# Two chained matmuls with a GELU: the first slices of b loaded by another queue, and the order of the first loads

## The chip, the cores and the metric

The kernel runs on one core of a Trainium2 chip. The metric is the device time of one execution in microseconds. Three runs of the kernel before gave 117.23, 117.33 and 117.46 us, so the median is 117.33.

Five engines work side by side, each through its own list of instructions: TensorE (PE, with its weight loads shown apart as PEld), VectorE (DVE), ScalarE (ACT), GpSimd (POOL) and SyncE (SP). Transfers from the chip's memory (DRAM) are issued by SP and POOL here, and moved by 16 DMA engines.

## The reference

```python
m, k, n, p = 1024, 1024, 2048, 1024
h = np.matmul(a, b)            # a: 1024 x 1024, b: 1024 x 2048, float32
h = 0.5 * h * (1 + np.tanh(np.sqrt(2 / np.pi) * (h + 0.044715 * h ** 3)))
return np.matmul(h, c).astype(np.float32)      # c: 2048 x 1024
```

## The kernel before

Everything is computed in bf16 or in a rounded fp32 form (FP32R) with fp32 sums in PSUM. The order of the work on each engine is written out by hand.

**Stages.** The first 512 columns of b are multiplied with a in the plain way: this is the loading stage, in which the data arrive (L114). The next 512 columns of b (`zero`), the last 1024 (`one`) and the whole second product with c (`two`) are each computed by a scheme with seven block products in place of eight (`Seven`, L212), whose sums and differences DVE forms (L170). GELU is applied by ACT as it takes the sums out of PSUM (L118).

**The loading stage.** a is needed transposed, with the contraction index on the partitions. It comes in pieces `a_part(h, q)`: h is the half of the rows, q one of four groups of 256 columns, 512 KB each in fp32. Of b's first 512 columns there are eight slices k, 256 KB each; `b_part(q)` is slices 2q and 2q + 1.

- `cast_a` (L128) casts a piece to bf16 with the engines it is given, each one share of the columns. `turn` (L138) transposes a piece, eight times 128 x 128 on PE by means of the matrix `ident` (L145), into PSUM, and DVE copies each of the two results into `aT` (L146). It is a generator: `next(tn)` does one half. `cast_b` (L149) casts a slice of b into `b1`, `block` (L156) issues the matmuls of L114, and `stir` (L122) issues matmuls on zeros, which nobody reads.
- SP issues, in this order: a(0,0) into `sta` (L75), b's slices 0 and 1 into `stb` (L76), a(1,0) (L77), a(0,1) (L78), b's slice 2 (L79). These arrive as fp32 and are cast by DVE and ACT.
- POOL first builds `ident` (L51), then copies one element of a(0,0) into `gate` (L81), which holds it until that piece has landed. Then it issues all other loads, which cast from fp32 to bf16 on the way: a(1,1) (L91), b's slice 3 (L92), a(0,2), b's slices 4 and 5, a(1,2), a(0,3), b's slices 6 and 7, a(1,3) (L86 and L89), then the rest of b (L98, L101) and c (L104). From the ninth on, each waits until the load eight places earlier has landed.
- ACT runs one GELU on a constant into the tile `g` (L82), so that its table is loaded early.

**The first work on PE** (L229 to L242): five stirs; the first half of a(0,0)'s transposes, a stir, the second half, a stir; then the matmuls of b's slice 0 with four column tiles and of slice 1 with two; then a(1,0)'s transposes, and so on. Between those, slices 0 and 1 of b are cast (L233, L236): slice 0 by DVE, DVE and ACT, slice 1 by ACT.

**The end.** The second product's results go out by `store` (L428), called in `done2` (L431); one tile of them goes out in two halves (L436).

Of the kernel before, what the change touches and what calls it, by code (L numbers as in the profile page):

```python
# [9 lines left out]
F32 = mybir.dt.float32  # L10
F32R = mybir.dt.float32r
BF16 = mybir.dt.bfloat16
AF = mybir.ActivationFunctionType
# [6 lines left out]
def kernel(ctx, tc, a, b, c, out):  # L20
    nc = tc.nc
    M, K = a.shape
    _, N = b.shape
    _, P = c.shape
    H = 512
# [8 lines left out]
    consts = ctx.enter_context(tc.tile_pool(name="consts", bufs=1))  # L34
# [5 lines left out]
    def slot(tag, shape, dt, name):  # L40
        return big.tile(shape, dt, name=name, tag=tag)

    def bank(i, shape=(128, H), dt=F32, name="ps"):
        return pp.tile(list(shape), dt, name=name, tag=f"bank{i}", padded_shape=None)

    def pieces(tag, bufs, shape, dt, name):
        return small.tile(shape, dt, name=name, tag=tag, bufs=bufs)

    warm = nc.const_aps.tensor(0.0, [128, 256], F32)
    ident = consts.tile([128, 128], BF16, name="ident")  # L50
    make_identity(nc, ident)  # L51
    gate = consts.tile([128, 1], F32, name="gate")
    g = consts.tile([128, 1], F32, name="g")

    consts.tile([128, 16], F32, name="room")

    c_sb = keep.tile([128, NT, P], BF16, name="c_sb")
    hT = [keep.tile([128, NT, H], BF16, name=f"hT{h}") for h in range(2)]
# [1 line left out]
    b1 = slot("b1", [128, KT, 1024], BF16, "b1")  # L60
# [4 lines left out]
    stb = slot("x0", [128, KT, H], F32, "stb")  # L65
    sta = slot("x1", [128, 2, 2, 4, 256], F32, "sta")
    abq = slot("x3", [128, 4, 2, 4, 256], BF16, "abq")

    def a_part(h, q):
        return av[:, 4 * h:4 * h + 4, ds(q * 256, 256)]  # L70

    def b_part(q):
        return bv[:, 2 * q:2 * q + 2, 0:H]

    nc.sync.dma_start(out=sta[:, 0, 0], in_=a_part(0, 0))  # L75
    nc.sync.dma_start(out=stb[:, 0:2], in_=b_part(0))  # L76
    nc.sync.dma_start(out=sta[:, 1, 0], in_=a_part(1, 0))  # L77
    nc.sync.dma_start(out=sta[:, 0, 1], in_=a_part(0, 1))  # L78
    nc.sync.dma_start(out=stb[:, 2], in_=bv[:, 2, 0:H])  # L79

    nc.gpsimd.tensor_copy(gate, sta[:, 0, 0, 3, 0:1])  # L81
    nc.scalar.activation(g, warm[:, 0:1], AF.Gelu_apprx_tanh)  # L82


    def cast_load_a(h, q):
# [13 lines left out]
    for n in range(2):  # L99
        for k in range(0, KT, 4):  # L100
            nc.gpsimd.dma_start(out=b2[:, k:k + 4, ts(n, H)],  # L101
                                in_=bv[:, k:k + 4, ds(1024 + n * H, H)])
# [3 lines left out]
    def copy(eng, dst, src):  # L106
        if eng is nc.scalar:
            nc.scalar.activation(dst, src, AF.Copy)
        else:
            nc.vector.tensor_copy(dst, src)  # L110
# [11 lines left out]
    def stir(*widths):  # L122

        for w in widths:
            nc.tensor.matmul(ps[0, 3][:, 0:w], warm[:, 0:128], warm[:, 0:w],
                             start=True, stop=True, skip_group_check=True)

    def cast_a(h, q, *engs):  # L128

        ab = pieces("ab", 2, [128, 4, 256], BF16, "ab")  # L130
        for i, eng in enumerate(engs):
            w = 256 // len(engs)
            for j, e in enumerate(eng if isinstance(eng, tuple) else (eng,)):
                m = slice(2 * j, 2 * j + 2) if isinstance(eng, tuple) else slice(0, 4)
                copy(e, ab[:, m, ts(i, w)], sta[:, h, q][:, m, ts(i, w)])
        return ab

    def turn(h, q, i, ab):  # L138

        banks = i if isinstance(i, tuple) else (i,)  # L140
        pts = [bank(x, (128, 2, H), BF16, "pt") for x in banks]
        for n in range(2):
            pt = pts[n % len(pts)]
            for m in range(4):
                nc.tensor.transpose(pt[:, n, ts(m, 128)], ab[:, m, ts(n, 128)], ident)  # L145
            nc.vector.tensor_copy(aT[:, h, 2 * q + n], pt[:, n])  # L146
            yield

    def cast_b(k, *engs):  # L149
        c0 = 0  # L150
        for i, eng in enumerate(engs):
            w = (H - c0) if i == len(engs) - 1 else H // len(engs) // 128 * 128
            copy(eng, b1[:, k, ds(c0, w)], stb[:, k, ds(c0, w)])
            c0 += w
# [72 lines left out]
    one = Seven(4, quarters(b2, 0, H), BB, [None] * 4, zero.t)  # L227

    stir(256, 256, 256, 256, 256)  # L229
    tn = turn(0, 0, 4, cast_a(0, 0, nc.vector))  # L230
    next(tn)
    stir(128)
    cast_b(0, nc.vector, nc.vector, nc.scalar)  # L233
    next(tn)
    stir(64)
    cast_b(1, nc.scalar)  # L236
    ab = cast_a(1, 0, nc.vector, nc.scalar)
    block(0, range(4), (0,))
    block(0, range(2), (1,))
# [9 lines left out]
    tn = turn(0, 1, 7, ab)  # L249
# [4 lines left out]
    for q in range(1, 3):  # L254
        k = 2 * q
        block(0, range(4), (k,))
        tn = turn(1, q, 7, abq[:, q, 1])
# [5 lines left out]
        tn = turn(0, q + 1, 7, abq[:, q + 1, 0])  # L263
# [10 lines left out]
    tn = turn(1, 3, 0, abq[:, 3, 1])  # L274
# [153 lines left out]
    def store(mt, q0, w, ot, eng=None):  # L428
        (eng or nc.sync).dma_start(out=out[ts(mt, 128), ds(q0, w)], in_=ot)

    def done2(i, l, j, p):  # L431
        if (i, l) == (1, 0):
            ot = pieces("o", 4, [128, H], F32, "ot")
            nc.vector.tensor_copy(ot, p)
            p = ot
        n = 2 if (i, l, j) == (0, 0, 1) else 1  # L436
        for q in range(n):
            r = ds(q * (H // n), H // n)
            store(4 * i + j, l * H + q * (H // n), H // n, p[:, r])

    def between2(n):
# [12 lines left out]
        elif n == "P73":  # L454
            two.t4(two.t[1], 4)

    seven(two, done2, between2)


# [28 lines left out]
```

## Time and profile before

| | |
|---|---|
| median of three runs | 117.33 us |
| the profiled execution | 117.6 us |
| its span, first to last instruction | 115.8 us |
| PE busy | 110.7 us, 96% of the span |
| DVE busy | 90.1 us, 78% |
| ACT busy | 51.4 us, 44% |
| POOL busy | 17.3 us, 15% |
| granted clock of TensorE | 1.00 throughout |
| read from DRAM, written to it | 20.97 MB, 4.19 MB |
| loads by SP and POOL, us from issue to landing | a(0,0), a(1,0) and a(0,1): 6.2 (median of the three); b's slices 0 and 1: 5.4; the five casting loads of a: 8.0 (median) |

Times in the profile are in microseconds from the start of the span. A busy PE says little, since matmuls are pipelined and their ends are modelled. What matters is where PE stands still, what released it, and when the loads that released it were issued and landed. The rate of the transfers in the profile counts bytes written: a load that casts from fp32 to bf16 reads twice what it writes. Queue q1 holds SP's transfers, q0 those of POOL, q8 fetches of instructions.

### The profile page before, as it was taken

To read this page: it belongs to the slowest core of one execution; us is meant where nothing else is said; L and a number is where in the kernel's file an instruction comes from. 1 tells how busy PE (TensorE), PEld (TensorE's weight loads), DVE (VectorE), ACT (ScalarE), POOL (GpSimd) and SP (SyncE) were. 2 spreads that over 40 slices of the span, in tenths; PEclk is the share of its full clock that TensorE was granted. 3 is DMA by queue.
4 is the path that set the end of the run, shared out by engine and by line. 5 is a ranking of instruction groups with operands and counts; after the bars stand their busy time and mean duration, and the time that the engine had idled before them with its cause. 6 is when DMAs were issued, how large, how long until landed. Compare 5 with 4: busy or idle time off the path is not lost.

```text
span 115.8 us, 1473 instructions
## 1 busy us (share of the span) xinstructions
PE 110.7 (96%) x544; PEld 77.1 (67%) x550; DVE 90.1 (78%) x108; ACT 51.4 (44%) x86; POOL 17.3 (15%) x29
## 2 busy tenths in 40 slices
PE   7889999999999999999999999999999999999990
PEld 6545555445777447888886444588888888888870
DVE  0247747689999998944789999999999986964581
ACT  5053000799268998066699339700043992000000
POOL 2497754222332000000000000000000000000000
PEclk9999999999999999999999999999999999999999
DMA  3999999999999999998000000070000002004994
GB/s 74 296 381 221 200 199 204 204 207 207 205 210 210 211 212 212 212 210 163 9 0 0 6 0 0 0 272 0 0 0 0 0 0 94 2 27 173 364 358 166
DMA packets 13414, 15.94 MB, mean 138 GB/s; under 512 B 736, under 2 KB 9184, under 8 KB 13408
## 3 DMA queue, kind: packets, MB, share of 16 engines
q0 software_dynamic: 8672, 9.31, 47.6%
q1 hardware_dynamic: 4592, 6.42, 15.7%
q10 hardware_dynamic: 144, 0.13, 0.3%
q8 instruction: 4, 0.07, 0.2%
q14 instruction: 2, 0.02, 0.0%
HBM read 20.97 MB, written 4.19 MB: 217 GB/s over the span
## 4 chain that ended last, share of the span: by engine, by line
PE 79%; DMA 13%; POOL 5%; issue 0%; DVE 0%
PE ps L212 76%; DMA abq<-in_a_dram 10%; DMA sta<-in_a_dram 3%; POOL abq L86 3%; PE ps L114 2%; POOL b L89 1%; POOL gate L81 1%; PE pt L145 1%; POOL b L92 0%; DVE ot L375 0%
## 5 line engine op out<-in xcount | busy, mean ns | idle before, releaser
L212 PE MATMUL ps<-x,s 128*128 128x512 f32 x128 | 29.6, 391 | 0.0
L212 PEld LDWEIGHTS ps<-x,s 128*128 128x128 f32 x128 | 24.0, 188 | 5.1
L212 PE MATMUL ps<-x,x 128*128 128x512 f32 x96 | 22.9, 394 | 0.0
L212 PEld LDWEIGHTS ps<-x,x 128*128 128x128 f32 x96 | 18.0, 188 | 3.9
L114 PE MATMUL ps<-aT,b 128*128 128x512 bf16 x62 | 15.7, 379 | 0.3 <-DVE b L110 0.2
L298 ACT ACTIVATE v<-ps 128x512 f32<-128x512 f32 x10 | 6.0, 598 | 19.1 <-PE ps L212 19.1
L212 PE MATMUL ps<-c_sb,hT 128*128 128x512 bf16 (+2 forms) x78 | 14.1, 336 | 0.1
L212 PE MATMUL ps<-x 128*128 128x512 f32 x56 | 13.2, 393 | 0.0
L212 PEld LDWEIGHTS ps<-x 128*128 128x128 f32 x56 | 10.2, 188 | 2.7 <-ACT u L298 0.4
L212 PEld LDWEIGHTS <-hT 128*128 128x128 bf16 x80 | 7.1, 98 | 7.0 <-issue 0.5
L118 ACT ACTIVATE hT<-ps 128x512 bf16<-128x512 f32 x14 | 7.3, 596 | 9.6 <-PE ps L114 9.6
L118 ACT ACTIVATE hT<-ot 128x512 bf16<-128x512 f32 x18 | 10.4, 623 | 2.1 <-DVE ot L303 2.0
L146 DVE COPY aT<-pt 128x512 bf16<-128x512 bf16 x16 | 6.7, 422 | 5.5 <-PE pt L145 5.4
L212 PE MATMUL ps<-aT,b 128*128 128x512 bf16 x46 | 10.6, 379 | 0.1
L303 DVE TENSOR_TENSOR ot<-ps,u 128x512 f32<-128x512 f32 x10 | 6.7, 688 | 5.2 <-ACT u L298 5.2
L303 DVE TENSOR_TENSOR ot<-ps,v 128x512 f32<-128x512 f32 x10 | 6.7, 688 | 4.9 <-DMA out_dram<-ot 3.9
L170 DVE TENSOR_TENSOR x<-c_sb 128x1024 fp32r<-128x1024 bf16 x8 | 9.2, 1216 | 0.0
L114 PEld LDWEIGHTS <-b 128*128 128x128 bf16 x64 | 5.7, 97 | 4.5 <-DVE b L110 0.3
L212 PEld LDWEIGHTS <-b 128*128 128x128 bf16 x48 | 4.6, 97 | 5.7 <-issue 0.3
L104 POOL DMA_DIRECT2D c_sb<-in_c_dram x8 | 5.6, 703 | 13.4 <-DMA b<-in_b_dram 11.1
L170 DVE TENSOR_TENSOR x<-b 128x1024 fp32r<-128x1024 bf16 (+1 forms) x4 | 7.0, 1751 | 0.6 <-issue 0.6
L298 ACT ACTIVATE u<-ps 128x512 f32<-128x512 f32 x10 | 5.9, 597 | 3.4 <-PE ps L212 3.2
(44 smaller groups left out, 110.7 us busy)
## 6 DMA issues: line engine op xcount, KB each, us to landing
c_sb<-in_c_dram POOLq DMA_DIRECT2D x8, 512.0 KB, 19.7
out_dram<-ot SPq DMA_DIRECT2D x14, 256.0 KB, 2.1
b<-in_b_dram POOLq DMA_DIRECT2D x6, 512.0 KB, 15.6
sta<-in_a_dram SPq DMA_DIRECT2D x3, 512.0 KB, 6.2
abq<-in_a_dram POOLq DMA_DIRECT2D x5, 256.0 KB, 8.0
stb<-in_b_dram SPq DMA_DIRECT2D x1, 512.0 KB, 5.4
b<-in_b_dram POOLq DMA_DIRECT2D x2, 256.0 KB, 8.3
stb<-in_b_dram SPq DMA_DIRECT2D x1, 256.0 KB, 7.2
```

The lines of the kernel that those rows point to most:

```text
L81: nc.gpsimd.tensor_copy(gate, sta[:, 0, 0, 3, 0:1])
L86: nc.gpsimd.dma_start(out=abq[:, q, h], in_=a_part(h, q))
L89: nc.gpsimd.dma_start(out=b1[:, 2 * q:2 * q + 2, 0:H], in_=b_part(q))
L104: nc.gpsimd.dma_start(out=c_sb[:, t:t + 2], in_=cv[:, t:t + 2])
L114: nc.tensor.matmul(p, b1[:, k, ts(t, 128)], aT[:, h, k], start=(k == 0), stop=(k == KT - 1))
L118: nc.scalar.activation(hT[h][:, t], p, AF.Gelu_apprx_tanh)
L145: nc.tensor.transpose(pt[:, n, ts(m, 128)], ab[:, m, ts(n, 128)], ident)
L146: nc.vector.tensor_copy(aT[:, h, 2 * q + n], pt[:, n])
L170: nc.vector.tensor_tensor(out=dst[:, r], in0=x[:, r], in1=y[:, r], op=op)
L212: nc.tensor.matmul(p[:, ds(c0, w)], l[:, k, ts(j, 128)], r[:, k, ds(c0, w)], start=(start and k == 0), stop=(k == self.kt - 1), skip_group ...
L298: nc.scalar.activation(st, p, AF.Copy)
L303: nc.vector.tensor_tensor(out=ot, in0=p, in1=st, op=ADD)
```

## The change

Slices 0 and 1 of b are no longer loaded by SP as fp32 and cast by DVE and ACT: POOL issues their load, with the cast, as its first instruction, ahead of `ident`. SP's second load is then a(1,0). ACT's early GELU writes its one element into the place that a(1,0) will fill, so that SP issues that load only when ACT is done; the tile `g` is gone, and `room` is one element larger. a(0,0) is cast half by DVE and half by ACT, its eight transposes follow each other into two banks of PSUM, and the two small stirs come behind them. Two of the tiles of the second product go out in halves instead of one.

```diff
-    make_identity(nc, ident)
     gate = consts.tile([128, 1], F32, name="gate")
-    g = consts.tile([128, 1], F32, name="g")
-
-    consts.tile([128, 16], F32, name="room")
+
+    consts.tile([128, 17], F32, name="room")
...
+    nc.gpsimd.dma_start(out=b1[:, 0:2, 0:H], in_=b_part(0))
+    make_identity(nc, ident)
     nc.sync.dma_start(out=sta[:, 0, 0], in_=a_part(0, 0))
-    nc.sync.dma_start(out=stb[:, 0:2], in_=b_part(0))
+    nc.scalar.activation(sta[:, 1, 0, 0, 0:1], warm[:, 0:1], AF.Gelu_apprx_tanh)
     nc.sync.dma_start(out=sta[:, 1, 0], in_=a_part(1, 0))
     nc.sync.dma_start(out=sta[:, 0, 1], in_=a_part(0, 1))
     nc.sync.dma_start(out=stb[:, 2], in_=bv[:, 2, 0:H])
 
     nc.gpsimd.tensor_copy(gate, sta[:, 0, 0, 3, 0:1])
-    nc.scalar.activation(g, warm[:, 0:1], AF.Gelu_apprx_tanh)
...
     stir(256, 256, 256, 256, 256)
-    tn = turn(0, 0, 4, cast_a(0, 0, nc.vector))
-    next(tn)
-    stir(128)
-    cast_b(0, nc.vector, nc.vector, nc.scalar)
-    next(tn)
-    stir(64)
-    cast_b(1, nc.scalar)
+    for _ in turn(0, 0, (4, 5), cast_a(0, 0, nc.vector, nc.scalar)):
+        pass
+    stir(128, 64)
     ab = cast_a(1, 0, nc.vector, nc.scalar)
...
-        n = 2 if (i, l, j) == (0, 0, 1) else 1
+        n = 2 if (i, l) == (0, 0) and j else 1
```

## The prediction

> **What bounds the kernel now.** I read the chain of waits first. It says that PE ends the span, and which transfer PE last waited for.
>
> ```profile
> 10.15 11.43 DMA abq<-in_a_dram
> 21.58 0.05 issue
> 21.63 0.40 PE pt L145 x4
> ...
> 73.79 39.11 PE ps L212 x188
> ```
>
> Columns: start, duration, what. Nothing but PE stands on the chain from 21.63 us on, with "issue" gaps of 0.05 us. The change moves nothing behind that point except one split store, so it must be read from when PE can start the transposes of a's last piece, abq(1,3), at 21.63.
>
> Next the timeline of the loading stage: start, duration, engine, line, and in brackets the idle time before and its releaser.
>
> ```profile
> 0.74 0.42 SPq L75 DMA_DIRECT2D sta<-in_a_dram  x1
> 1.77 0.46 SPq L77 DMA_DIRECT2D sta<-in_a_dram  x1
> 2.04 0.20 ACT L82 ACTIVATE g<-const-float32-0.0 128x1 f32<-128x1 f32 x1
> 4.46 0.69 DVE L110 CAST ab<-sta 128x1024 bf16<-128x1024 f32 x1 [4.46 <-DMA sta<-in_a_dram]
> 5.14 0.88 POOL L86 DMA_DIRECT2D abq<-in_a_dram  x1
> 6.62 0.94 ACT L108 ACTIVATE b<-stb 128x256 bf16<-128x256 f32 x2 [4.38 <-DMA stb<-in_b_dram]
> 6.90 1.47 PE L114 MATMUL ps<-aT,b 128*128 128x512 bf16 x6 [0.17 <-DVE b L110]
> 7.99 0.43 DVE L110 CAST ab<-sta 128x512 bf16<-128x512 f32 x1 [0.68 <-DMA sta<-in_a_dram]
> 7.99 0.63 ACT L108 ACTIVATE ab<-sta 128x512 bf16<-128x512 f32 x1 [0.44 <-DMA sta<-in_a_dram]
> 8.47 0.62 PE L145 MATMUL pt<-ident,ab 128*128 128x128 bf16 x8
> 15.99 0.24 PEld L145 LDWEIGHTS <-abq 128*128 128x128 bf16 x4 [0.30 <-DMA abq<-in_a_dram]
> 21.62 0.23 PEld L145 LDWEIGHTS <-abq 128*128 128x128 bf16 x4 [0.64 <-DMA abq<-in_a_dram]
> ```
>
> PE's first real matmul is at 6.90. Two later places show PE waiting for data that this change does not reorder: abq(1,2) at 15.99 (PE had just become free, no loss) and abq(1,3) at 21.62. Single starts put PE's last matmul before the second at 21.10; at the pace of 0.217 us between them PE was free at 21.32, so this wait costs 0.31 us.
>
> So **an earlier start of PE alone is worth nothing**: PE would arrive earlier at 15.99 and 21.62 and wait for the same landings. Only a load stream that ends earlier moves the end. Third, then, the stretches: length, five engines busy (count), PE's clock, DMA share, GB/s written.
>
> ```profile
> 2.50:4.25 1.75, 1.75 (x6) 1.37 (x6) 0.00 (x0) 0.00 (x0) 0.00 (x0) 1.00 1.09 347
> 4.25:5.50 1.25, 0.82 (x8) 0.42 (x6) 0.69 (x1) 0.00 (x0) 1.01 (x2) 1.00 0.87 238
> 6.00:8.50 2.50, 2.10 (x13) 1.07 (x13) 1.19 (x5) 1.45 (x3) 2.50 (x5) 1.00 1.08 384
> 10.00:19.00 9.00, 8.90 (x68) 5.06 (x70) 5.89 (x13) 0.72 (x2) 5.51 (x9) 1.00 1.38 199
> ```
>
> From 10 us on POOL's queue casts fp32 to bf16, so 199 written is 398 read. The stream runs at 384 to 398 read from about 2.5 to the end, except for a **dip** to 238 between 4.25 and 5.50: it loses 1.25 x (384 - 238)/384 = 0.48 us. The packets of the dip are those of b's first two slices (2 KB each, SP's queue).
>
> **The change part by part.**
>
> *b's first slices through POOL's queue.* Removed: SP's issue (L76, 0.50 us) and the four casts of L110 and L108 (DVE 0.36, ACT 0.94). Added: one POOL issue ahead of ident; L89 has the same shape and takes 0.73. POOL goes through it from 0.74 to 1.47, and ident's two instructions (0.57 us from 0.74 before) end near 2.1. Their user is the first transpose, near 4.9: covered by 2.8 us. The gate still waits for sta(0,0), and the first cast load behind it was issued at 5.14 and sent no packet until 8.8: covered by over 3 us. POOL now has nine loads ahead of L98, and the ninth, abq(1,3), waits for b's landing; it was issued at 10.15, by when b has landed in every case below.
>
> When b lands is not shown. Its first packet has two bounds: SP's first issue (0.74) gave packets at 1.83, so 1.09 us later; POOL's first (5.14) gave them at 8.82, 3.68 later, behind SP's packets. So 1.83 to 4.42. I take about 2.5, nearer SP's row, because POOL's contains the wait behind others. If packets go out in the order in which they were issued, b lands as before at 6.59, or 0.5 earlier without the dip. No cast follows: first matmul at 6.65 or 6.15 instead of 6.90. The wait added is that of PE's first weight load of L114 for this load; all of PE's later work is queued behind it.
>
> *a's first piece cast by DVE and ACT.* 0.69 on DVE becomes 0.43 beside ACT's 0.63 (rows at 7.99). In that row PE's first matmul on new data (9.39) is 1.42 behind the landing (7.97). sta(0,0) lands at 4.44, so aT is ready at 5.86; the two stirs, now behind all eight transposes, end near 6.1. Again b decides. Worth nothing alone.
>
> *a's second piece behind ACT's warm-up.* L77 moves from 1.77 to 2.24 + 0.06 = 2.30; L78 and L79 behind it go 0.53 later too. First packets at 2.30 + 1.09 = 3.39. sta(0,0)'s packets went out until 4.0, so the stream has no hole: cost nothing. Were the cover gone, the hole would cost at most 0.53. DVE's and ACT's casts of sta(1,0) are what would start late then.
>
> *The split store.* SP issues one store more (about 0.5 us) near 77 us, where it waits for DVE anyway (100.5 us of waits in six). Nothing.
>
> *Sum.* The stream moves the same bytes read in the same order. Ends: at 398 instead of 384 the 0.52 MB of b take 1.31 instead of 1.36 us, so 0.05 less with the dip kept; 0.48 + 0.05 = 0.53 less with it gone. Below nothing: the stretch in which SP's and POOL's packets ran together, 8.8 to 10.2, moved 0.18 MB cast (0.36 read) and 0.14 plain, 0.50 in 1.4 us or 357 read; over the 2.6 us that b and a would share, that loses about 0.2.
> I take 0.45 less: the dip's packets are all of the load that leaves SP's queue, and reads of the same 2 KB from the same tensor by POOL's queue ran at 398 with no dip. PE can follow: it needs 0.45 and gets 0.25 to 0.75 at the first matmul, 0.5 at sta(1,0), and has the 0.31. The profiled execution took 117.6 (span 115.8 and 1.8 around it); less 0.45 it is 117.15. The median of the runs is 0.27 lower, 117.33, so the forecast is **116.9**. What this kernel's measurement can tell from no change is about 0.2%, 0.23 us.
>
> Two rules of the Trainium skill, page "DMA: Bandwidth & Descriptors", bear on this. Section "Issuing engines are not separate DMA queues" speaks against the change: loads of all issuers share the same engines, and a second issuer saves only issue time; by it the gain is 0.05. Section "Queues, rings and completion order" says that an engine alternates between queues that have work. The trace differs: from 6.0, when POOL's first issue was over, until 8.8 only SP's packets went out.
>
> ```profile
> q1 hardware_dynamic: 1214, 1.35, 104.3%
> ```
>
> That is the only data queue in 5.0 to 8.8 (packets, MB, share).
>
> **Rivals.**
>
> 1. *SP's packets go first* (slower). That row can also mean that POOL's packets start only when SP's queue is empty, not that they follow in order of issue. Then b waits for sta(0,0), sta(1,0), sta(0,1) and stb's third slice. Without stb(0:2), which took 2.15 (4.44 to 6.59), SP's queue would be empty at 10.07 - 2.15 = 7.9; b then takes 1.3 and lands at 9.2. First matmul 9.25, 2.35 late; PE makes up the 0.31 at 21.3 and some 0.5 of stalls (8.21 to 8.47, 11.15 to 11.37), so 1.5 remain: **118.9**. It decides once b lands later than 6.84 + 0.8 = 7.6. For it: the row. Against: the order of issue explains the same row, and here b is issued ahead of the second a.
>
> 2. *Fair sharing* (slightly slower). b and sta(0,0) share from 2.5 on. sta(0,0) has 0.45 MB left at half of 350 GB/s, so lands near 5.4 instead of 4.44, and the first matmul is at 5.4 + 1.42 = 6.8 or, with b shared until 7, at 7.1. That alone is free; the stream loses the 0.2 of mixing, and what else starts late adds up to 0.4: **117.7**.
>
> 3. *The dip stays* (no change). stb's third slice, 2 KB packets on SP's queue as well, shows no dip at 8.5 to 9.2, and the dip may belong to that time and not to that load. Then abq(1,3) lands 0.05 earlier: **117.3**. The earlier start of PE is lost at 15.99.
>
> **How the numbers follow.** Forecast (116.4 to 117.05) 0.50; dip stays 0.20; fair sharing 0.12; SP first 0.18. The range leaves out SP first and little else: from 116.4 (0.53 less; 0.3 less again if POOL's packets fill the stretch from 2.0 to 2.5, which moved 123 GB/s where 350 followed; 0.1 of scatter) to 118.2 (rival 2 and half of the way to rival 1). Faster 0.50, within 0.2% 0.20, slower 0.12 + 0.18 = 0.30.
>
> **What will show it.** Right: the first L114 matmul between 6.1 and 6.7, no stretch under 300 GB/s before 6 us (cast bytes counted double), the last abq landing near 21.1, PE unbroken behind it. SP first: LDWEIGHTS of L114 waits for b's load until about 9 while sta(1,0) lands near 6.6, and PE waits nowhere at 15.99 or 21.6. Fair sharing: the first cast starts behind 5. Dip stays: first matmul early, but longer waits for abq near 16 and 21.6. Wrong altogether: a changed time behind 21.6, where the code is the same; a 16 KB instruction fetch at 19.57, which held back the last of abq(1,3)'s sixteen increments (fifteen had come by 19.92, the last at 21.58), may fall behind that landing instead and move the end by up to 0.3 by itself.

## The result, and the profile after

The changed kernel took **119.92 us** in the median of six runs, between 118.17 and 122.25; the kernel before took 117.30 in the median of six runs beside them (117.21 to 117.62). The ratio is **1.0115 (95% interval 1.0086 to 1.0144)**: slower by about 1%; by the medians of all six it is 1.022. The ratio counts only the three runs within 1.5% of the fastest (118.17, 118.27 and 119.54), since slower ones are usually left out as disturbed; here, as the experiments show, the spread belongs to the kernel. The forecast was 116.9, in a range of 116.4 to 118.2.

The profiled execution took 120.29 us (span 118.5, against 115.8). Its chain of waits no longer goes through a's last piece, but through b's first load (start, duration, what):

```profile
1.23 7.25 DMA b<-in_b_dram
8.48 0.05 issue
8.53 2.50 PE ps L113 x6
11.04 0.85 PE pt L144 x8
```

Behind this it is all PE. (Line numbers of the changed kernel are up to five lower than those of before.) The timeline of the same execution:

```profile
0.74 0.44 SPq L75 DMA_DIRECT2D sta<-in_a_dram  x1
1.23 0.83 POOL L73 DMA_DIRECT2D b<-in_b_dram  x1 [0.78 <-POOLq L467]
2.26 0.38 SPq L77 DMA_DIRECT2D sta<-in_a_dram  x1
4.38 0.43 DVE L109 CAST ab<-sta 128x512 bf16<-128x512 f32 x1 [4.38 <-DMA sta<-in_a_dram]
5.18 0.72 PE L144 MATMUL pt<-ident,ab 128*128 128x128 bf16 x8
8.53 0.33 PEld L113 LDWEIGHTS <-b 128*128 128x128 bf16 x3 [2.32 <-DMA b<-in_b_dram]
8.53 2.50 PE L113 MATMUL ps<-aT,b 128*128 128x512 bf16 x6 [2.18 <-DMA b<-in_b_dram]
10.83 1.06 PE L144 MATMUL pt<-ident,ab 128*128 128x128 bf16 x8
```

a(0,0) lands and is cast as forecast, the transposes are done before 6 us, and then PE stands still for 2.18 us until b has landed at 8.48. The first six matmuls then take 2.50 us where they took 1.47, and eight transposes 1.06 for 0.62. The reason stands in the stretches (length, five engines busy, granted clock, DMA share, GB/s written):

```profile
2.50:3.75 1.25, 1.25 (x4) 0.98 (x4) 0.00 (x0) 0.00 (x0) 0.14 (x1) 1.00 1.06 366
3.75:5.00 1.25, 1.25 (x4) 0.84 (x4) 0.43 (x1) 0.62 (x1) 0.59 (x2) 1.00 1.07 136
5.00:6.25 1.25, 1.25 (x13) 1.03 (x11) 0.53 (x2) 0.01 (x1) 1.25 (x3) 1.00 0.65 110
8.50:11.75 3.25, 3.22 (x15) 1.74 (x16) 0.88 (x2) 1.14 (x3) 2.00 (x3) 0.55 1.27 277
```

PE's clock is 0.55 on the mean from 8.50 to 11.75: it was 0.50 from 8.82 to 12.23, one period of 3.41 us, and 1.00 before and behind. And the slow stretch of the stream is not gone but has grown: only 110 GB/s written from 5.00 to 6.25, with the engines at 0.65. Between 3.75 and 5.00 nearly all packets are b's cast ones (157 of 175), so 136 written is some 270 read; from 5.00 to 6.25 they are half b's and half a(1,0)'s (68 and 77), and 110 written is some 160 read.

**Where the 2.70 us of this execution come from.** a's last transposes start at 24.33, before at 21.63. The first matmul is 8.53 - 6.90 = 1.63 late. From there to the transposes of a(0,1), at 13.04 for 10.03, another 1.38 are lost, in a stretch for most of which the clock was halved. And the wait of 0.31 for a(1,3) is gone, as PE comes later than that load: 1.63 + 1.38 - 0.31 = 2.70.

### The profile page after: what moved, and what is told of

It reads as the page before. It is cut to its first block, busy times and chain, and to the rows that moved or that the text cites. A ratio compares the mean times of both kernels' runs of the same rounds, so it can differ in the third digit from the quotient of the medians.

```text
span 118.5 us, 1478 instructions
## 1 busy us (share of the span) xinstructions
PE 112.6 (95%) x550; PEld 78.3 (66%) x550; DVE 89.5 (76%) x106; ACT 51.1 (43%) x85; POOL 17.7 (15%) x30
## 4 chain that ended last, share of the span: by engine, by line
PE 90%; DMA 6%; issue 1%; DVE 0%; POOLq 0%
PE ps L211 74%; PE ps L113 13%; DMA b<-in_b_dram 6%; PE pt L144 3%; DVE ot L370 0%; POOLq L467 0%; POOLq masks.py:199 0%
## 5 line engine op out<-in xcount | busy, mean ns | idle before, releaser
L113 PE MATMUL ps<-aT,b 128*128 128x512 bf16 x64 | 17.4, 403 | 2.2 <-DMA b<-in_b_dram 2.2
L211 PE MATMUL ps<-aT,b 128*128 128x512 bf16 x48 | 10.7, 379 | 0.0
L109 DVE CAST ab<-sta 128x512 bf16<-128x512 f32 (+1 forms) x4 | 1.7, 440 | 7.3 <-DMA sta<-in_a_dram 7.3
```

What stands on the lines that cost most here:

```text
L113: nc.tensor.matmul(p, b1[:, k, ts(t, 128)], aT[:, h, k], start=(k == 0), stop=(k == KT - 1))
L211: nc.tensor.matmul(p[:, ds(c0, w)], l[:, k, ts(j, 128)], r[:, k, ds(c0, w)], start=(start and k == 0), stop=(k == self.kt - 1), skip_group ...
```

## The experiments

Each changes the kernel named; ratios are against the kernel before, on the same chip. The letters are those of the expectations: Q, the use of POOL's queue alone makes the loss; S, packets of another queue hold b's back; C, b's reads are slow there; T, that time is slow; D, POOL's later issues hold b back; K, PE's clock; L, the order of SP's last waits; P, only POOL's queue is served late; R, other parts of the change cost. My theory after the result was that b's load on POOL's queue is held back by SP's a(1,0) (Q with S), and that the clock doubles the price (K); the rivals are the other letters.

**b_by_sp and b_by_sp2: everything except the queue.** The changed kernel, with

```diff
-    nc.gpsimd.dma_start(out=b1[:, 0:2, 0:H], in_=b_part(0))
...
     nc.sync.dma_start(out=sta[:, 0, 0], in_=a_part(0, 0))
+    nc.sync.dma_start(out=stb[:, 0:2], in_=b_part(0))
...
+    cast_b(0, nc.vector, nc.vector, nc.scalar)
     stir(128, 64)
+    cast_b(1, nc.scalar)
```

> All of the change except the queue: b's first slices again by SP behind a(0,0), and cast by DVE and ACT; a(1,0) held back for ScalarE, a(0,0) cast by two engines, the stirs and the split store stay. Theory Q (POOL's queue alone makes the loss): 117.3, within 0.3 us of before, b landing near 6.6, first L113 matmul 6.7 to 6.9, clock 1.00. Rival R (the later a(1,0) or the stirs behind the transposes cost): 117.8 or more, with a(1,0) landing behind 8.3.

118.00 (ratio 1.0063, 1.0041 to 1.0085): neither. Yet its profile had a's last transposes at 21.59, 0.04 earlier than before; the difference came behind PE's last instruction, 3.6 us for 3.15. b_by_sp2 goes back to one tile in halves as well:

```diff
-        n = 2 if (i, l) == (0, 0) and j else 1
+        n = 2 if (i, l, j) == (0, 0, 1) else 1
```

> As b_by_sp, but with one tile less stored in halves, so that SP issues as many transfers as in the kernel before. Theory L (the last waits of SP go round eight semaphores in turn, and one more transfer shifts which comes first; b_by_sp's profile ended 3.6 us behind PE's last matmul, before's 3.15): 0.4 below b_by_sp, 117.5 to 117.6, the end 3.15 behind PE. Rival: 118.0 as b_by_sp.

**117.26, ratio 1.0000 (0.9989 to 1.0012).** So all parts but the queue, taken together, cost and bring nothing, and Q holds. The first matmuls stand where they stood before, and wait for the cast of b, as it lands at 6.57:

```profile
6.93 1.47 PE L113 MATMUL ps<-aT,b 128*128 128x512 bf16 x6 [0.43 <-DVE b L109]
```

 The 0.74 between the two is theory L's, of which the waits of SP's queue at the end show 0.5: first b_by_sp, then b_by_sp2 (us in total, times, longest).

```profile
SPq L480 <- DMA out_dram<-ot: 1.2, 1, 1.2
```

```profile
SPq L480 <- DMA out_dram<-ot: 0.7, 2, 0.4
```

In b_by_sp the first of SP's eight closing waits for stores is for the very last store, which landed at 114.90, and the seven behind it follow one after another, 0.06 us each; in b_by_sp2 the last store is waited for last, and five of the waits are over before the three late stores land. The semaphores of these transfers are used in turn, eight of them, and b_by_sp has 25 transfers (one of them ScalarE's) where the kernel before and the changed one have 24: the split store of the change keeps the number as it was, and so this order.

**pool_holds: POOL's other loads held until b has landed.**

```diff
     nc.gpsimd.tensor_copy(gate, sta[:, 0, 0, 3, 0:1])
+    nc.gpsimd.tensor_copy(gate, b1[:, 1, 0:1])
```

> The changed kernel, with POOL's other loads held back until b's first slices have landed. Theory D (writing the next loads' descriptors holds up the packets of b): b lands near 5.5 to 6, time 117.5 or less. Theories S and C: b lands at 7 to 8.5 as before, first matmul 7 to 8.5, and the time stays at 118 to 122 with a wide spread.

121.74 (1.0366), b landing at 9.34: D falls. (The time is longer mainly because the held loads come later; only b's landing speaks on D.)

**a10_after_b and b_alone: SP's a(1,0) held until b has landed**, in b_alone POOL's other loads too (the line of pool_holds).

```diff
+    nc.scalar.activation(sta[:, 1, 0, 0, 0:2], b1[:, 0:2, 0], AF.Copy)
     nc.sync.dma_start(out=sta[:, 1, 0], in_=a_part(1, 0))
```

> The changed kernel, with a(1,0) issued only when b's first slices have landed (ScalarE writes the element from b). Theory S (SP's packets of a(1,0) hold b's back on the DMA engines): b lands near 5.5, as its first seven of sixteen engines did in the profile of the changed kernel; a(1,0) then near 8. Rival C (the reads of b are slow there whoever shares the engines) or rival D (POOL's own later issues): b lands at 7.5 or later all the same, and the time is 121 or more.

b landed at 6.32, earlier than in any other profile with POOL's load, though not at the 5.5 expected:

```profile
1.23 5.09 DMA b<-in_b_dram
```

 The time, 127.9 (1.0898), comes from a(1,0), which now lands at 15.96 among POOL's loads, where 8 was expected.

> The changed kernel, in which neither SP nor POOL issues another load until b's first slices have landed. Theory S: all of b by 6.4 us again, as in a10_after_b. If b's reads or POOL's queue are slow by themselves: 7.5 or later. The time says nothing (over 120), since the engines stand idle behind it.

A single run, 122.09: b landed at 6.92, later than 6.4 and earlier than 7.5, so S is only half right. With nothing else on the engines the load has a tail (the columns as above):

```profile
3.75:5.00 1.25, 1.25 (x4) 0.84 (x4) 0.43 (x1) 0.00 (x0) 0.44 (x1) 1.00 1.13 166
5.00:6.25 1.25, 0.81 (x5) 0.36 (x3) 0.41 (x1) 0.00 (x0) 0.00 (x0) 1.00 0.22 35
```

166 written, 332 read, until 5.00, and then 35, with the engines at 0.22: by the sixteen increments with which each load in the trace reports its landing, taken here as one for each of the sixteen DMA engines, thirteen had their share by 5.6 and the last three were done at 5.97, 6.71 and 6.92. In the changed kernel seven were done by 5.5, and the last four at 7.09 to 8.48. A few engines are late with b by themselves, and later still beside a(1,0). The trace's records of single packets say by what. In b_alone a packet of b takes 98 ns and the next one on its engine starts 79 ns after it, but 8 of the 256 took over 200 ns, the longest 866: an engine that meets such packets falls behind. In the changed kernel 19 took over 200 ns, the longest 847; and of the 36 b packets that start after 6.3 us, 29 have another one some 133 ns behind, which leaves room for one of a(1,0)'s packets (46 ns) between. I read this as a late engine giving b every other turn; the records do not name the engine. Why single reads take so long is not shown.

**pe_busy: PE given work while it waits.**

```diff
-    stir(128, 64)
+    stir(128, 64, 256, 256, 256, 256, 256)
```

> The changed kernel with five more stirs of 256 columns (0.43 us each, 2.1 us) behind the last ones, so that PE does not stand still while it waits for b. Theory K (part of the loss and most of the spread is PE's clock, halved for one 3.41 us period behind one in which PE stood still for 2.2 us): clock 1.00 in every run, 118.2 to 118.8 with a narrow spread. Rival (the spread comes from when b lands): still 118 to 122.

119.39 (118.75 to 120.13), ratio 1.0171, clock 0.998 to 1.00 in all four. The clock part holds and the spread is 1.4 us instead of 4.1; in the changed kernel the three runs with a mean clock of 0.996 or more took 118.17 to 119.54, and the three at 0.972 to 0.984 took 120.29 to 122.25. But the time is above the forecast of K: in the profile b landed as late as 9.35, and PE still stood 0.74:

```profile
9.39 0.82 PE L113 MATMUL ps<-aT,b 128*128 128x512 bf16 x3 [0.74 <-DMA b<-in_b_dram]
```

 The added stirs also end only at 8.65, so where b lands earlier they hold PE themselves. From the first matmul to the transposes of a(0,1) this profile took 3.50 (9.39 to 12.89), 0.45 of it a wait for a(0,1); the kernel before took 3.13, and the changed kernel 4.51 under the halved clock. By these two profiles the clock was worth about 1.0 of the 1.38. K is part of the spread; the rest I put down to b's landing, of which each kernel has one profile.

**b_first: SP's first two loads exchanged** in the kernel before.

```diff
-    nc.sync.dma_start(out=sta[:, 0, 0], in_=a_part(0, 0))
     nc.sync.dma_start(out=stb[:, 0:2], in_=b_part(0))
+    nc.sync.dma_start(out=sta[:, 0, 0], in_=a_part(0, 0))
```

> The kernel before, with SP's first two loads exchanged: b's slices first, then a(0,0). Theory C (the slow stretch of 4.2 to 5.5 us belongs to the first reads of b's rows): the rate drops while b's 2 KB packets go out, 2 to 4 us, and not at 4.2 to 5.5. Rival T (it belongs to that time): the drop stays at 4.2 to 5.5, in a's packets. Time by both 117.5 to 118.5, since the casts wait in another order.

120.54 (1.031), later than both expected, as a(0,0) lands at 6.83 and PE stands for 2.7 us. The stretches answer the question (the first holds the start of the stream; the kernel before, with a's packets there, had 283 in it):

```profile
2.00:3.75 1.75, 1.75 (x5) 1.39 (x5) 0.00 (x0) 0.22 (x2) 0.00 (x0) 1.00 0.84 198
3.75:5.00 1.25, 1.14 (x4) 0.59 (x3) 0.00 (x0) 0.00 (x0) 0.00 (x0) 1.00 0.94 278
5.00:6.25 1.25, 0.00 (x0) 0.00 (x0) 0.00 (x0) 0.83 (x2) 0.00 (x0) 1.00 1.07 374
```

While b's packets go out, up to 5 us, the rate is 198 to 278; from 5.00 on a's packets run at 374, which the old dip (4.25 to 5.50) did not reach. T falls: through SP's queue the slow stretch goes with b's first two slices.

**touch and after_touch: b's rows read ahead.** The kernel before and the changed one, with

```diff
+    nc.scalar.dma_start(out=room[:, 0:2], in_=bv[:, 0:2, 0])
     nc.sync.dma_start(out=sta[:, 0, 0], in_=a_part(0, 0))
```

and one tile less stored in halves.

> The kernel before, with one small load ahead of all others, issued by ScalarE: four bytes of each of b's first 256 rows (into an unused tile); one store goes out whole, so that the number of transfers is the same. Theory C (first reads of memory rows not read before are slow): no stretch below 300 GB/s at 4.2 to 5.5, b lands at 6.1 instead of 6.6 and the stream ends 0.4 earlier; 116.8 to 117.0. Rival T: the stretch stays, 117.2 to 117.6.

117.47, ratio 1.0018 (0.9992 to 1.0044): nothing gained. b landed at 6.41 for 6.59, and the stretch from 4.25 to 5.50 still ran at 247, for 238 before.

> The changed kernel with the same small load of b's rows ahead, and one store less in halves. Theory C: POOL's load of b runs at over 300 GB/s read from its first packet at 3.7 on, so it has landed before a(1,0)'s packets come at 5; b lands at 5.5, time 116.8 to 117.3, clock 1.00. Rival S alone or T: b lands at 7 to 9 as in the changed kernel, 118 to 121.

117.78 (117.65 to 118.33), ratio 1.0046 (1.0016 to 1.0076). This is the best of the kernels in which POOL loads b, but not as C has it: its profile, of the slowest run, shows b at 7.77. The touch also makes ScalarE's warm-up, and with it a(1,0), 0.5 us later, hence the next two.

**hold, hold4, ungated: a(1,0) issued at 2.78, 3.39 and 1.23** instead of 2.26. The first two make the warm-up longer (2 and 4 GELUs of 128x256), the third lets it write elsewhere:

```diff
-    nc.scalar.activation(sta[:, 1, 0, 0, 0:1], warm[:, 0:1], AF.Gelu_apprx_tanh)
+    for i in range(2):
+        nc.scalar.activation(sta[:, 1, 0, i], warm, AF.Gelu_apprx_tanh)
```

> The changed kernel with a(1,0) issued some 0.5 us later (ScalarE's warm-up is two wider GELUs), and nothing touched ahead: SP's issue is as late as in after_touch. Theory S (sharing with a(1,0)): the gain of after_touch was this delay, so 117.8 to 118.2. Rival C (the touch of b's rows made it): 118.2 to 122 as the changed kernel.

> As hold with four wider GELUs: a(1,0) issued near 3.7, first packets near 4.8. Theory S: b lands at 5.5 to 6.5 in most runs, first matmul at 6.2 to 6.6, but a(1,0) is later; 117.4 to 117.9. Rival: b's own rate varies whoever shares, b lands at 7 to 9 and the time is over 118.

> The changed kernel with a(1,0) not held back for ScalarE (the warm-up writes elsewhere): SP issues it at 1.2, a microsecond earlier. Theory S: b lands at 8.5 or later, first matmul behind 8.5, 119.5 to 122. Rival (the hold itself costs, by leaving the engines short of work): 117.5 to 118.

118.98 (1.0155), 119.05 (1.0159) and 119.23 (1.0197): all alike, b landing at 7.55, 7.79 and 8.39. So the delay doesn't explain after_touch; the touch itself is worth about 1.2 us there (118.98 - 117.78), and how is open. In hold and hold4 a(1,0)'s first packets go out near 5.0, as in the changed kernel, whenever SP issues it; in ungated, where its issue ends before POOL's, its packets go out from 3.73 to 5.39, and b's only from 4.97 on. The engines start these loads in the order of issue, as the forecast had it. The hold therefore does what it is for, and buys nothing that these runs can tell.

**b_by_act and act_late: b on ScalarE's queue**, as fp32, with the rest as in b_by_sp2.

```diff
-    nc.sync.dma_start(out=stb[:, 0:2], in_=b_part(0))
+    nc.scalar.dma_start(out=stb[:, 0:2], in_=b_part(0))
```

> All of the change except POOL's queue: b's first slices are issued by ScalarE's own queue at 0.74, as fp32, beside SP's a(0,0), and cast by DVE and ACT as in b_by_sp2. Theory S in its general form (any two queues share an engine, and some engines finish the older load late): a(0,0) lands near 5, b at 6.5 to 7.5; 117.5 to 118.5. Rival P (only POOL's queue is served late): b lands at 6.0 to 6.6, 117.0 to 117.4.

> As b_by_sp2, but b's first load is issued by ScalarE behind its warm-up, at 2.24, while SP issues a(1,0) at 2.26: a second hardware queue in the place of POOL's. If any second queue makes b late (theory S: its packets alternate with those of a(1,0), as those of a(0,0) did in b_by_act): b lands at 7 to 8.5, a(1,0) about as late, 118 to 119.5. If only POOL's queue does: b lands by 6.7, 117.2 to 117.6.

119.68 (1.0211) and 119.83 (1.0216). act_late missed its aim: ScalarE issued the load at 0.80, past the table load and the GELU ahead of it, so it repeats b_by_act. In b_by_act the two loads share the engines evenly, between 3.0 and 4.5 (packets, MB, share):

```profile
q10 hardware_dynamic: 189, 0.39, 70.9%
q1 hardware_dynamic: 193, 0.20, 37.1%
```

One packet of b (q10) goes out for each of a(0,0) (q1), together 390 GB/s; behind that the rate fell to 264, from 4.50 to 5.00. b landed at 6.12, as P expects, but a(0,0) only at 6.39 instead of 4.44, which is S's way, though S had it near 5; PE then waits for a. This is the forecast's second rival, seen between two other queues.

**nocast and a10_pool: what POOL loads.** nocast has POOL load b as fp32 into `stb`, cast as before. In a10_pool b comes by SP and POOL's first load is a(1,0), cast on the way into a free part of `abq`:

```diff
+    nc.gpsimd.dma_start(out=abq[:, 0, 1], in_=a_part(1, 0))
     make_identity(nc, ident)
...
-    nc.sync.dma_start(out=sta[:, 1, 0], in_=a_part(1, 0))
...
-    ab = cast_a(1, 0, nc.vector, nc.scalar)
+    ab = abq[:, 0, 1]
```

> The changed kernel with POOL's first load of b as fp32 into the staging tile, cast by DVE and ACT as before. If the cast on the way makes it late: b lands by 6.6 and the time is 117.3 to 117.8. If POOL's queue beside SP's does: b lands at 7.5 to 9.4 all the same, 118.5 to 120.

> b's first slices by SP as before, and POOL's first load is a(1,0), with the cast; SP's a(0,1) is held back for ScalarE. If POOL's queue is served late whatever it carries: a(1,0) lands at 8.5 to 9.5, behind the 8.0 of before, 118 to 119.5. If b's reads are the trouble: a(1,0) lands by 8 and spares the casts, 116.9 to 117.4.

nocast: 120.89 (1.026), b at 9.03: the cast on the way is not what makes b late. a10_pool: 117.33, ratio 1.0007 (0.9993 to 1.0021), in which a(1,0) lands at 8.83: fourteen engines were done by 7.84, two at 8.50 and 8.83. PE waits 0.52 for it and is at a's last transposes at 21.78, only 0.15 behind the kernel before. So POOL's first load lands late here too, though less (7.97 before), and whether that costs depends on what waits for it. No kernel beats the one before.

## Why the prediction was wrong

**The step that failed is "When b lands".** The forecast took the first packet at 2.5 and the landing at 6.15 to 6.6. The first packet went out at 3.68: inside the bounds (1.83 to 4.42), though not near the end I chose. That was no loss: in the kernel before, b's first packet of 2 KB went out at 3.66, behind a(0,0)'s, so the order of issue held, and that POOL reached its issue at 1.23 instead of 0.74 does not show in it. Nor did b's reads take more of the engines' time: its 256 packets add up to 31.3 us over the sixteen, against 30.1 before and 32.2 in b_by_sp2. What failed is the step from there to the landing: a load has landed when the slowest of sixteen engines has its share. Through SP's one queue the sixteen ended within 0.83 us (5.76 to 6.59); through POOL's they spread over 3.2 (5.32 to 8.48), as an engine that was late with b took a(1,0)'s packets in turn (b_alone). The end is 7.5 to 9.4 in all profiles in which POOL loads b and SP's other loads are beside it. The first rival's price, 118.9, came near (1.0115 of 117.30 is 118.65), but that was luck: its mechanism (SP's packets first) was not what happened in the changed kernel. Its crossing point, b at 7.6, was too generous: in hold b landed at 7.55 and 118.98 came of it, because SP's loads were late as well (a(0,1) at 11.21 for 9.37), and PE waited for them too.

**The dip was read wrongly.** I took it to go with SP's queue because later 2 KB reads on POOL's queue ran at full rate. b_first shows that through SP's queue it goes with b's first two slices, and through POOL's the rate fell further, to some 160 GB/s read for 1.25 us, mixed from b's and a(1,0)'s packets. Nor does it belong to those slices alone: beside a(0,0), in b_by_act, 189 of their 256 packets went out from 3.0 to 4.5, at 390 GB/s in all. The rows of before also held more than one dip: they gave 347 from 2.50 to 4.25 and 318 from 5.50 to 6.00, not the 384 that the sum took for all but the dip. The two pieces of evidence weighed against each other, POOL's later full rate and stb's third slice, both spoke of other slices of b.

**The stream.** That an earlier PE alone is worth nothing was not put to the test. The other way round it held in part: the 0.31 at a's last piece took up that much of the loss.

**A cost that was not in the sum: PE's clock.** No term or rival had it, though a rival with PE standing still for two microseconds was there; it was worth about 1.0 us of the 2.70. The Trainium skill ("TensorE: Matmul & The Clock Gate", "Part 1: The HAM clock gate") says that the clock is judged in windows of 3413 ns that run on regardless of the kernel, and halved behind an idle one; the trace has just such a period of 3.413 us at 0.50. But the window ahead of it was not idle: PE had worked 1.24 of its 3.41 us, and the measurement decides.

**Right:** a(0,0)'s cast, the stirs and the held a(1,0) (no hole): together worth nothing, by b_by_sp2. ident behind POOL's issue was done at 2.64 in the changed kernel's profile, and the first transpose came at 5.18: covered. The split store was put at nothing as an issue; it is worth 0.7 by what it keeps (theory L), as the change takes one transfer from SP and the split gives it back.

**The rule that spoke against the change.** The Trainium skill's rule that issuers do not add bandwidth ("DMA: Bandwidth & Descriptors", "Issuing engines are not separate DMA queues") stood up: no kernel with b on a second queue was faster. The same page's rule that an engine alternates between queues ("Queues, rings and completion order"), which I set aside for the row at 6.0 to 8.8, is what b_by_act shows packet for packet (189 against 193), where both loads were issued together, and what b's late packets show beside a(1,0)'s in the changed kernel.

**What stays open.** Why single reads of b's first rows take up to 0.87 us, so that some engines are slow with them (alone on POOL's queue the last was done 1.3 us behind the thirteenth); why loads that were issued further apart followed one another where b_by_act's alternated; and why a read of four bytes of each row, which did nothing for SP's load, took 1.2 us off the time with POOL's. Neither the cast, nor POOL's later issues, nor the time of a(1,0)'s issue is the cause; with SP's packets beside it b landed 0.6 to 2.4 us later than alone (7.55 to 9.35 for 6.92; 6.32 in a10_after_b), in single profiles.

## What to carry to other kernels

A load that the first work waits for did best here in one queue with the loads that follow it: there its sixteen shares ended within 0.83 us, while in a queue of its own the one engine that was late and shared the longest set the landing. Look at the spread of a load's increments, and not only at the bytes and the order. And a wait early in a kernel is to be priced with the clock behind it: two microseconds of standing still cost about another microsecond here.

## What the runs showed of the hardware

- PE's clock went to a half for a period of 3.41 us when PE had stood still for 1.89 us or more of the period of 3.41 us ahead of it (a10_after_b 1.89, act_late 1.96, the changed kernel 2.18, pool_holds 2.36, nocast 2.49, b_first 2.72), and not at 1.69 or less (b_alone 1.69, b_by_act 1.45, ungated 1.43, hold4 1.38). The periods count, not the gap: in b_alone PE stood for 1.98 us on end, of which 1.55 fell into one period.
- SP's closing waits follow a fixed order, 0.06 us each where the store has landed; one transfer more in the kernel moved the end by 0.5 us in the profile and 0.74 in the median.
- A spread between the engines stays: in the changed kernel every casting load up to a's last piece landed with a spread of about 1.65 us over the sixteen engines (19.60 to 21.24 for the last), where before it was 0.7 (19.24 to 19.92, without one increment at 21.58, behind an instruction fetch at 19.57).
- ScalarE issued a load past its own table load and GELU: in act_late at 0.80, while the table load ran from 0.73 to 2.0.
- Two loads that SP and ScalarE issued together alternated packet for packet (b_by_act, 189 against 193 packets in 1.5 us). In ungated, SP's and POOL's issues both began at 1.23, SP's ended 0.33 earlier, and its load's packets went ahead: 3.73 for 4.97.
